# A planner that books VectorE's and GpSimd's shared memory ports, in a two-layer hybrid decoder step on one core

## The chip, the cores and the metric

The kernel runs on one core of one Trainium2 chip. The core has five engines, each with an instruction queue of its own that it works off in order: TensorE (PE in the profile; its weight loads are PEld), VectorE (DVE), ScalarE (ACT), GpSimd (POOL) and SyncE (SP), which here issues nearly all DMAs. Engines wait for each other through semaphores. SBUF is the memory that all of them read and write; PSUM holds TensorE's results. The metric is the device time of one execution in microseconds.

## The reference, cut to what matters

One inference step of two layers, for a prompt of 2048 rows (1024 wide, float32) and for 8 samples with a paged cache of 2048 earlier rows each. The weights are shared.

```python
# layer 0 (even): spatial gating || stick-breaking attention
h = x @ w_in_even;  u, v, gate_a, q, k, vb, gate_b = split(h)
out_a = gelu(u) * (tril(w_sp) @ standardize(gelu(v)) + b_sp) * silu(gate_a)       # chunks of 128 rows
z = q @ k.T / 8;  att = sigmoid(z) * exp(sum of log_sigmoid(-z) over later keys)  # keys < query
out_b = (att @ vb) * silu(gate_b)
# layer 1 (odd): indexer-selected attention || multi-scale pooling
h = x @ w_in_odd; q, kv, q_idx, k_idx, w_idx, gate_c, p, gate_d = split(h)
index = sum_h relu(q_idx[h] @ k_idx.T) * w_idx[h];  sel = top_k(index, 256)        # per query row
out_c = softmax(q @ k[sel].T / 8 + rel_bias) @ v[sel] * silu(gate_c)
out_d = ((mean of p over the last 2, 4, 8, 16 rows - p) @ w_grp) * scale * silu(gate_d)
# both layers
x = layer_norm(alpha * x + concat(out_1, out_2) @ w_out, g, b)
```

It returns both sets of rows and the new cache entries.

## The kernel before

**The work.** The prompt is cut into four blocks of 512 rows. Every projection is made in three matmuls of split operands (high x high, low x high, high x low: L671 to L673, and L1066 to L1068 for the output projection). The splits are made on the chip: ScalarE copies the high half (L597, L584) and a subtraction gives the low half. For the weights (`load_w`, L592) GpSimd subtracts the first half of the columns and VectorE the second, both after the same copy (L600). Stick-breaking attention (`b_logits`) runs its product along the keys as a scan on VectorE (L975); where the layers overlap, GpSimd turns a tanh into a sigmoid (L966) and masks the diagonal (L971). Sparse attention (`c_logits`) adds a mask to the logits and takes their maximum in one VectorE instruction that reads PSUM (L1705), and GpSimd prepares a piece of that mask (L1690). The selection (`topk`) is a search in six rounds for each 128 query rows: counts over the whole row on ScalarE and VectorE (L1449, L1451), and between them some dozen VectorE instructions of one to eight elements (L1482 to L1499), each of which needs the one before. Layer norm scales on ScalarE (L1148), multiplies on GpSimd (L1149) and adds on VectorE (L1150). The samples' work is spread among all of that.

**The order.** `Body.run` writes the instructions in an order woven by hand from these pieces. The class `Order` then throws this order away and plans its own for each of the five queues. `gather` (L154) collects what depends on what and which tiles share a buffer. `cost` (L243) gives each instruction the time that it keeps its engine and the time until its result is there: from the table `BUSY`, by engine, output tile, operation and size, or else from a formula. `plan` (L407) simulates the chip: whenever an engine is free it takes the ready instruction of the lowest rank, and a result is seen by others `SEM` ns later. `latest` (L499) walks the finished plan backwards and gives the latest time at which each could start, which is the rank for the next plan. `settle` (L316) repeats that for each of three guesses, plays each plan through under a few drawn sets of durations (`draw` L341, `replay` L356) and keeps the one with the least sum. `keep` (L554) fixes it:

```python
for o in self.order.values():
    for a, b in zip(o, o[1:]):
        self.tc.add_manual_dep(self.ins[b], self.ins[a].name, info, reason="planned order")
```

`o` is one engine's order and `info` a dependency without a semaphore, so the plan's times are not enforced: each engine starts its next instruction as soon as its own waits are over. The planner before knows nothing of the ports that VectorE and GpSimd share. Its table holds what instructions took in a profile, with whatever delayed them.

Of the kernel before, what the change touches and what calls it, by code (L numbers as in the profile page):

```python
# [12 lines left out]
F32R = mybir.dt.float32r  # L13
# [6 lines left out]
PSUM = bass.MemoryType.PSUM  # L20
DRAM = bass.MemoryType.DRAM

P = 128
# [35 lines left out]
    "ACT g_s Activation 512": 515, "ACT s16 TensorCopy 128": 150, "ACT s_sg Activation 8": 95,  # L59
    "ACT zt Activation 128": 390, "ACT zt Activation 256": 500, "ACT zt Activation 384": 605,  # L60
    "DVE P TensorScalarPtr 256": 655, "DVE P TensorScalarPtr 384": 900, "DVE bf TensorCopy 1": 50,
    "DVE bfst TensorCopy 4": 145, "DVE fq TensorReduce 4": 60, "DVE fq TensorScalarPtr 1": 65,
    "DVE hT TensorCopy 8": 80, "DVE halo TensorCopy 16": 400, "DVE ix TensorScalarPtr 128": 465,
    "DVE ix TensorScalarPtr 256": 540, "DVE ix TensorScalarPtr 512": 810, "DVE kid TensorCopy 512": 345,
    "DVE kid TensorTensor 512": 640, "DVE ln_nb TensorScalarPtr 4": 70, "DVE ln_rs TensorTensor 1": 405,
    "DVE mk TensorScalarPtr 640": 940, "DVE mv BNStatsAggregate 6": 80, "DVE mx TensorScalarPtr 512": 665,
    "DVE nmax TensorReduce 1": 65, "DVE nmax TensorReduce 2": 70, "DVE nmax TensorReduce 3": 70,
    "DVE nmax TensorReduce 4": 70, "DVE nmax TensorReduce 5": 70, "DVE os_ TensorTensor 2": 225,
    "DVE os_ TensorTensor 4": 70, "DVE pg TensorTensor 512": 680, "DVE pl TensorScalarPtr 512": 835,
    "DVE pl TensorTensor 16": 410, "DVE ri Reciprocal 4": 90, "DVE rs_a TensorScalarPtr 4": 275,  # L70
    "DVE rs_t TensorScalarPtr 1": 60, "DVE rs_t TensorScalarPtr 4": 285, "DVE rs_t TensorTensor 1": 385,
    "DVE rs_t TensorTensor 3": 65, "DVE rs_t TensorTensor 4": 100, "DVE s_acc TensorTensor 8": 75,
    "DVE s_cd TensorScalarPtr 8": 115, "DVE s_cd TensorTensor 24": 125, "DVE s_lg TensorTensor 128": 210,
    "DVE s_mxp TensorReduce 1024": 1995, "DVE s_pl TensorReduce 120": 1190, "DVE s_pl TensorTensor 8": 390,
    "DVE s_pr TensorScalarPtr 128": 730, "DVE s_qb TensorScalarPtr 8": 285, "DVE s_rq TensorScalarPtr 8": 110,
    "DVE s_sg TensorScalarPtr 8": 75, "DVE s_sgm TensorScalarPtr 128": 390, "DVE s_tmp TensorTensor 408": 560,
    "DVE s_tr Memset 8": 40, "DVE s_u TensorTensor 8": 125, "DVE s_xm TensorScalarPtr 8": 620,
    "DVE tk_M TensorTensor 8": 170, "DVE tk_W TensorTensor 3": 110, "DVE tk_a TensorScalarPtr 1": 245,
    "DVE tk_b TensorScalarPtr 1": 65, "DVE tk_b1 TensorScalarPtr 1": 95, "DVE tk_b2 TensorScalarPtr 1": 125,
    "DVE tk_f TensorScalarPtr 1": 120, "DVE tk_f TensorTensor 1": 190, "DVE tk_fl TensorCopy 1": 55,  # L80
    "DVE tk_mg TensorScalarPtr 1": 65, "DVE tk_mv TensorScalarPtr 2": 500, "DVE tk_nn TensorScalarPtr 2": 110,
    "DVE tk_oh TensorTensor 4": 160, "DVE tk_okn TensorScalarPtr 5": 210, "DVE tk_pen TensorScalarPtr 3": 315,
    "DVE tk_sd TensorScalarPtr 1": 65, "DVE tk_sd TensorTensor 1": 180, "DVE tk_th TensorScalarPtr 1": 235,
    "DVE tk_tn TensorCopy 2": 305, "DVE tk_tn TensorReduce 16": 85, "DVE tk_tn TensorScalarPtr 3": 400,
    "DVE tk_u TensorScalarPtr 1": 130, "DVE tk_u3 TensorScalarPtr 3": 265, "DVE tk_wd Reciprocal 1": 75,
    "DVE vT TensorCopy 1": 65, "DVE va TensorScalarPtr 512": 580, "DVE vea0 TensorCopy 4": 965,
    "DVE vea2 TensorCopy 4": 530, "DVE vlast TensorCopy 1": 65, "DVE xres TensorTensor 512": 1045,
    "DVE xs_ln TensorTensor 512": 600, "POOL P TensorScalarAffineSelect 128": 415,
    "POOL P TensorScalarPtr 256": 420, "POOL P TensorScalarPtr 384": 530, "POOL dT TensorTensor 512": 1240,
    "POOL ix TensorScalarAffineSelect 128": 405, "POOL nm TensorTensor 128": 600,  # L90
    "POOL ol TensorTensor 512": 1360, "POOL s_tr TensorTensor 8": 260, "POOL tk_W TensorScalarPtr 1": 485,
    "POOL tk_b2 TensorScalarPtr 1": 385, "POOL tk_f TensorScalarPtr 1": 190, "POOL tk_isl TensorTensor 1": 205,
    "POOL tk_u TensorScalarPtr 1": 260, "POOL ws TensorTensor 513": 1875, "POOL ws TensorTensor 521": 1190,
    "POOL ws TensorTensor 525": 1205, "POOL ws TensorTensor 527": 1050,
    "POOL wsp TensorScalarAffineSelect 128": 255, "POOL xres TensorTensor 512": 1520,
# [3 lines left out]
class Order:  # L99
# [5 lines left out]
    GUESSES = ((1.0, 150), (1.05, 150), (1.0, 0))  # L105
    ROUNDS, DRAWS, SPREAD = 5, 2, 0.12
    TAIL = {"ACT": 100, "POOL": 60, "DVE": 75}
# [135 lines left out]
    def cost(self, n):  # L243
# [38 lines left out]
        if e == "POOL":  # L282
            c = {"TensorTensor": 150 + (2.85 if i.outs[0].dtype == F32R else 2.4) * k, "Iota": 50 + 0.9 * k, "Memset": 40}.get(i.opcode, 330 + 0.9 * k)
            return c, c + 60
        if getattr(i, "is_tensor_tensor_scan", False):
            c = 130 + 2.3 * k
        elif k <= 16:
            c = 120 if len(full) < 2 and i.opcode != "TensorScalarPtr" else 190
        elif i.opcode == "TensorTensor" and not ps:
            c = 140 + 1.3 * k  # L290
        elif i.opcode == "TensorScalarPtr" and len(i.outs) > 1 and len(full) == 1:
            c = 150 + 1.05 * k
        elif i.opcode == "TensorScalarPtr" and not ps:
            c = 180 + 0.54 * k if len(full) == 1 else 160 + 1.1 * k
        else:
            c = 85 + 1.04 * k
# [18 lines left out]

    def settle(self):  # L316
# [7 lines left out]
        self.kinds = [self.kind(n) for n in range(N)]  # L324
        self.succ = [[] for _ in range(N)]
# [2092 lines left out]
```

## Time and profile before

| | |
|---|---|
| time, median of 3 runs | 2931.59 us (2930.24 to 2943.6) |
| the profiled execution | 2930.72 us, its span 2929.0 us |
| TensorE busy | 2726.8 us (93%) |
| VectorE busy | 2137.6 us (73%) |
| ScalarE busy | 1605.6 us (55%) |
| GpSimd busy | 1195.7 us (41%) |
| granted TensorE clock, mean | 0.970 |

The profile is of one execution. Busy time counts from an instruction's start to its end as the hardware recorded them. An instruction that has started and is then held up counts as busy, so VectorE's and GpSimd's busy time holds what they spend waiting for each other's ports. TensorE's matmuls overlap and their ends are modelled; its idle time is the time in which none runs. "PE z_c L1703 <- DVE mx L1705: 27.0, 15, 8.0" in the view of waits says that matmuls of line 1703, writing z_c, were held up 15 times by VectorE's instruction of line 1705, 27.0 us in all and 8.0 at most. The groups give busy us and mean ns of one, then the idle time of the engine before them and who ended it. The clock is the share of full speed that the chip granted TensorE; 0.5 is half speed.

### The profile page before, as it was taken

The numbers are of one execution on the slowest core, as the hardware profiler recorded it, in microseconds if no ns is written. First come the engines' busy times: TensorE is split into PE (matmuls) and PEld (weight loads), VectorE is DVE, ScalarE is ACT, GpSimd is POOL, SyncE is SP. The second block draws the span as 40 slices with busy tenths as digits, with TensorE's granted clock in tenths as the row PEclk, the third lists the DMA queues.
The fourth block names the chain that finished last, engine by engine and source line by source line (L and its number), as shares of the span: only waits on it lengthen the run. The fifth ranks groups of instructions, "written<-read, shape, count | busy, mean of one in ns | idle before, by whom it ended". The sixth has DMA issues, their size and how long they took to land. (4 is left out here: it accounts for less than half of the span.)

```text
span 2929.0 us, 52271 instructions
## 1 busy us (share of the span) xinstructions
PE 2726.8 (93%) x17490; PEld 2162.6 (74%) x17490; DVE 2137.6 (73%) x5297; ACT 1605.6 (55%) x3216; POOL 1195.7 (41%) x1300
## 2 busy tenths in 40 slices
PE   8999999989999999989799999998999999998986
PEld 6886777757767777668477667777767788887875
DVE  2376559756766977538887978887888877988865
ACT  2433334434444354435566677775776667776853
POOL 2223336422323543245453624446422555445342
PEclk9999999999999999989899999999989999998998
DMA  7556866775585668453475545435565655766452
GB/s 216 163 178 201 264 192 208 220 251 181 175 247 174 220 197 295 137 161 117 143 212 142 156 132 154 122 91 146 154 184 156 197 176 166 232 210 196 122 191 68
DMA packets 536591, 523.50 MB, mean 179 GB/s; under 512 B 43183, under 2 KB 408904, under 8 KB 536287
## 3 DMA queue, kind: packets, MB, share of 16 engines
q1 hardware_dynamic: 526439, 484.29, 55.2%
q0 software_dynamic: 9856, 35.66, 3.8%
q8 instruction: 138, 2.26, 0.3%
q14 instruction: 158, 1.29, 0.1%
HBM read 430.27 MB, written 89.73 MB: 178 GB/s over the span
## 5 line engine op out<-in xcount | busy, mean ns | idle before, releaser
L600 POOL TENSOR_TENSOR wl<-wr,wh 128x512 fp32r<-128x512 f32 x260 | 414.3, 1594 | 888.5 <-ACT wh L597 777.4
L671 PE MATMUL pp<-xh,wh 128*128 128x512 f32 (+1 forms) x1536 | 631.4, 414 | 23.0 <-DVE q_hl L590 9.1
L672 PE MATMUL pp<-xl,wh 128*128 128x512 f32 (+1 forms) x1536 | 617.7, 403 | 5.7 <-DVE xl L590 5.7
L673 PE MATMUL pp<-xh,wl 128*128 128x512 f32 (+1 forms) x1536 | 616.8, 402 | 0.7 <-POOL wl L600 0.7
L597 ACT CAST wh<-wr 128x1024 fp32r<-128x1024 f32 x260 | 269.9, 1038 | 383.4 <-PE pp L672 168.2
L600 DVE TENSOR_TENSOR wl<-wr,wh 128x512 fp32r<-128x512 f32 x260 | 222.3, 855 | 202.3 <-ACT wh L597 187.7
L671 PEld LDWEIGHTS pp<-xh,wh 128*128 128x128 f32 (+1 forms) x1536 | 288.7, 189 | 99.6 <-issue 19.8
L672 PEld LDWEIGHTS pp<-xl,wh 128*128 128x128 f32 (+1 forms) x1536 | 290.0, 189 | 68.6 <-issue 12.3
L673 PEld LDWEIGHTS pp<-xh,wl 128*128 128x128 f32 (+1 forms) x1536 | 289.5, 188 | 68.4 <-issue 10.1
L1066 PE MATMUL pp_o<-wh,oh 128*128 128x256 f32 x1008 | 295.9, 297 | 17.1 <-ACT oh L584 11.6
L975 DVE TENSOR_TENSOR_SCAN P<-P,bfst 128x512 f32<-128x512 f32 x192 | 275.0, 1441 | 28.3 <-ACT P L968 23.1
L1068 PE MATMUL pp_o<-wh,ol 128*128 128x256 f32 x1008 | 288.5, 291 | 4.0 <-POOL ol L590 4.0
L1067 PE MATMUL pp_o<-wl,oh 128*128 128x256 f32 x1008 | 290.9, 291 | 0.3 <-POOL wl L600 0.3
L1703 PE MATMUL z_c<-ksc,qc 128*128 128x512 f32 (+3 forms) x816 | 226.3, 358 | 37.9 <-DVE mx L1705 27.0
L999 ACT COPY P<-ps_p 128x512 f32<-128x512 f32 (+1 forms) x320 | 165.7, 522 | 156.3 <-PE ps_p L998 144.1
L1721 ACT ACTIVATE zt<-zt,nmax 128x512 f32<-128x512 f32 (+3 forms) x320 | 209.0, 655 | 57.3 <-DVE nmax L1709 56.4
L1066 PEld LDWEIGHTS pp_o<-wh,oh 128*128 128x128 f32 x1008 | 194.7, 194 | 27.7 <-ACT oh L584 12.6
L1736 ACT COPY zt<-ps_pc 128x512 f32<-128x512 f32 (+3 forms) x320 | 163.3, 519 | 88.4 <-PE ps_pc L1734 83.6
L961 PE MATMUL z<-ks,q 128*128 128x512 f32 (+3 forms) x640 | 196.2, 390 | 14.0 <-ACT r L1396 3.0
L1449 ACT ACTIVATE mk<-ix,tk_tn 128x512 int8<-128x512 f32 (+13 forms) x140 | 183.3, 1309 | 35.3 <-DVE tk_tn L1499 16.6
L1068 PEld LDWEIGHTS pp_o<-wh,ol 128*128 128x128 f32 x1008 | 193.3, 194 | 10.2 <-POOL ol L590 5.5
L1067 PEld LDWEIGHTS pp_o<-wl,oh 128*128 128x128 f32 x1008 | 195.6, 194 | 5.2 <-issue 1.8
(456 smaller groups left out, 5830.4 us busy)
## 6 DMA issues: line engine op xcount, KB each, us to landing
pg<-cache_b_kv SPq DMA_DIRECT2D x256, 256.0 KB
wr<-w_in_even SPq DMA_DIRECT2D x112, 512.0 KB
wr<-w_in_odd SPq DMA_DIRECT2D x76, 512.0 KB
wr<-w_out SPq DMA_DIRECT2D x68, 512.0 KB
ks<-ksc SPq DMA_DIRECT2D x80, 256.0 KB
ksc<-kcs SPq DMA_DIRECT2D x80, 256.0 KB
q<-qsc SPq DMA_DIRECT2D x64, 256.0 KB
qc<-qcs SPq DMA_DIRECT2D x128, 128.0 KB
```

Of the source, the lines that this page charges most:

```text
L597: nc.scalar.copy(hi, raw)
L600: e.tensor_tensor(lo[:, c], raw[:, c], hi[:, c].bitcast(F32), op=OP.subtract)
L671: nc.tensor.matmul(ps[:m], wh[:, kt, :m], xh[kt], start=a, stop=False)
L672: nc.tensor.matmul(ps[:m], wh[:, kt, :m], xl[kt], start=False, stop=False)
L673: nc.tensor.matmul(ps[:m], wl[:, kt, :m], xh[kt], start=False, stop=b)
L961: nc.tensor.matmul(z[:, :n], q2[:, c, t * P:(t + 1) * P].bitcast(F32R), ks[:, :n].bitcast(F32R), start=c == 0, stop=c == 1)
L975: nc.vector.tensor_tensor_scan(r, r, r, initial=ini, op0=OP.mult, op1=OP.bypass)
L1066: nc.tensor.matmul(ps[:, :256], oh[:, tt], wh[:, k], start=a, stop=False)
L1067: nc.tensor.matmul(ps[:, :256], oh[:, tt], wl[:, k], start=False, stop=False)
L1068: nc.tensor.matmul(ps[:, :256], ol[:, tt], wh[:, k], start=False, stop=b)
L1703: nc.tensor.matmul(z[:, :n], q2[:, c, jj % 2, :].bitcast(F32R), kk, start=c == 0, stop=c == 1)
L1721: nc.scalar.activation(zt, zt, AF.Exp, bias=nmx, accum_out=st["rs"][:, h, c:c + 1])
```

## The change

`port` is new. It says of each VectorE and GpSimd instruction whether it needs the shared ports: on GpSimd, whatever reads SBUF; on VectorE, what reads two tensors from SBUF (scans too), and copies and tensor-with-scalar operations from SBUF to SBUF with one output and more than one element. `plan` and `replay` keep a time `hold` for each of the two engines, up to which its running port instruction has the ports (its busy time less 60 ns). A port instruction of the other engine does not start before it. In `plan` the engine may take a ready instruction that needs no ports instead, if that ends at most 100 ns after the hold does.

The table and the formulas of `cost` are refitted to undisturbed durations; most small entries go away, since the formulas now cover them. `GUESSES` varies the hand-over time of the plan (200, 250 and 230 ns, the last with costs 4% up) where it varied costs and the price of a change between kinds of matmul. The replay, which still hands over in 200 ns, draws durations with a spread of 5% (12% before) and DMA times up to 1.15 (1.5 before). `settle` now keeps the `after` links (which tile follows which in a buffer) of the plan that it keeps.

No instruction is added or taken away, and the class `Body` is unchanged.

```diff
--- before.py
+++ after.py
@@ -56,43 +56,30 @@
 
 
 BUSY = {
...
-    "DVE mk TensorScalarPtr 640": 940, "DVE mv BNStatsAggregate 6": 80, "DVE mx TensorScalarPtr 512": 665,
...
-    "DVE tk_oh TensorTensor 4": 160, "DVE tk_okn TensorScalarPtr 5": 210, "DVE tk_pen TensorScalarPtr 3": 315,
...
-    "DVE vT TensorCopy 1": 65, "DVE va TensorScalarPtr 512": 580, "DVE vea0 TensorCopy 4": 965,
-    "DVE vea2 TensorCopy 4": 530, "DVE vlast TensorCopy 1": 65, "DVE xres TensorTensor 512": 1045,
...
-    "POOL P TensorScalarPtr 256": 420, "POOL P TensorScalarPtr 384": 530, "POOL dT TensorTensor 512": 1240,
-    "POOL ix TensorScalarAffineSelect 128": 405, "POOL nm TensorTensor 128": 600,
...
+    "ACT zt Activation 512": 710, "DVE P TensorScalarPtr 384": 840, "DVE bfst TensorCopy 4": 80,
...
+    "DVE tk_wd Reciprocal 1": 75, "DVE zt ISA 128": 210, "DVE zt ISA 256": 345,
+    "POOL P TensorScalarAffineSelect 128": 255, "POOL dT TensorTensor 512": 1000,
+    "POOL ix TensorScalarAffineSelect 128": 255, "POOL nm TensorTensor 128": 390,
+    "POOL s_tr TensorTensor 8": 155, "POOL tk_W Memset 1": 60, "POOL tk_W TensorScalarPtr 1": 250,
...
 }
 
 
@@ -102,9 +89,10 @@
     ENGINES = {"PE": "PE", "DVE": "DVE", "Activation": "ACT", "Pool": "POOL", "SP": "SP"}
     SEM, DMA_START, DMA_END, RATE = 200, 700, 1500, 280.0
     TILED = 150
-    GUESSES = ((1.0, 150), (1.05, 150), (1.0, 0))
-    ROUNDS, DRAWS, SPREAD = 5, 2, 0.12
-    TAIL = {"ACT": 100, "POOL": 60, "DVE": 75}
+    GUESSES = ((1.0, 200), (1.0, 250), (1.04, 230))
+    ROUNDS, DRAWS, SPREAD = 5, 2, 0.05
+    TAIL = {"ACT": 100, "POOL": 45, "DVE": 75}
+    OTHER, RELEASE, SLACK = {"DVE": "POOL", "POOL": "DVE"}, 60, 100
 
     def __init__(self, tc, lags):
         self.tc, self.lags = tc, lags
@@ -280,20 +268,17 @@
             c = 70 + (0.82 if ps else 0.87) * k if i.opcode == "TensorCopy" else 70 + 0.83 * k if ps else 200 + 0.93 * k
             return c, c + 100
         if e == "POOL":
-            c = {"TensorTensor": 150 + (2.85 if i.outs[0].dtype == F32R else 2.4) * k, "Iota": 50 + 0.9 * k, "Memset": 40}.get(i.opcode, 330 + 0.9 * k)
-            return c, c + 60
+            c = {"TensorTensor": 15 + 2.4 * k, "Iota": 50 + 0.9 * k, "Memset": 40}.get(i.opcode, 180 + 0.78 * k)
+            return c, c + 45
+        ptr = sum(getattr(x, "bass_ap", None) is not None and self.size(x) == 1 for x in i.ins) if k > 1 else 0
         if getattr(i, "is_tensor_tensor_scan", False):
-            c = 130 + 2.3 * k
-        elif k <= 16:
-            c = 120 if len(full) < 2 and i.opcode != "TensorScalarPtr" else 190
-        elif i.opcode == "TensorTensor" and not ps:
-            c = 140 + 1.3 * k
-        elif i.opcode == "TensorScalarPtr" and len(i.outs) > 1 and len(full) == 1:
+            c = 40 + 2.23 * k
+        elif i.opcode == "TensorScalarPtr" and not ps and len(full) == 1 and len(i.outs) == 1:
+            c = 65 + 0.54 * k + 60 * ptr
+        elif i.opcode == "TensorScalarPtr" and len(i.outs) > 1:
             c = 150 + 1.05 * k
-        elif i.opcode == "TensorScalarPtr" and not ps:
-            c = 180 + 0.54 * k if len(full) == 1 else 160 + 1.1 * k
         else:
-            c = 85 + 1.04 * k
+            c = 65 + 1.04 * k + 60 * ptr
         return c, c + 75
 
     def out(self, n):
@@ -312,6 +297,23 @@
             return None
         return "t" if i.is_transpose else "h" if self.halves(n) else "r" if i.ins[0].dtype == F32R else "f"
 
+
+    def port(self, n):
+
+        i, e = self.ins[n], self.eng[n]
+        if e not in self.OTHER or "DMA" in i.opcode or type(i).__name__ == "BassTileConditionalBlock":
+            return False
+        sb = lambda x: self.space(x) not in (None, DRAM, PSUM)
+        ins = [x for x in i.ins if getattr(x, "bass_ap", None) is not None]
+        full = [x for x in ins if self.size(x) > 1]
+        if e == "POOL":
+            return any(map(sb, ins))
+        if i.opcode == "TensorTensor" or getattr(i, "is_tensor_tensor_scan", False):
+            return sum(map(sb, ins)) > 1
+        if i.opcode == "TensorScalarPtr" and len(full) > 1:
+            return sum(map(sb, full)) > 1
+        return (i.opcode in ("TensorScalarPtr", "TensorCopy") and len(i.outs) == 1 and self.size(i.outs[0]) > 1
+                and all(map(sb, (*full, i.outs[0]))))
 
     def settle(self):
 
@@ -322,27 +324,32 @@
             self.costs[g] = busy, busy + 170
         self.dma = [e is not None and "DMA" in i.opcode for e, i in zip(eng, self.ins)]
         self.kinds = [self.kind(n) for n in range(N)]
+        self.ports = [self.port(n) for n in range(N)]
         self.succ = [[] for _ in range(N)]
         for n, d in enumerate(self.dep):
             for m in d:
                 self.succ[m].append(n)
         self.links()
         draws, mid, best = [self.draw(k) for k in range(self.DRAWS)], self.costs, None
-        for by, self.TILED in self.GUESSES:
+        sem = self.SEM
+        for by, near in self.GUESSES:
             self.costs = [(b * by, l * by) if e in self.TAIL else (b, l) for e, (b, l) in zip(eng, mid)]
+            self.SEM = near
             self.plan(list(range(N)))
             for _ in range(self.ROUNDS):
+                self.SEM = near
                 self.plan(self.latest())
+                self.SEM = sem
                 x = sum(self.replay(c) for c in draws)
                 if best is None or x < best[0]:
-                    best = x, self.order
-        self.costs, self.order = mid, best[1]
+                    best = x, self.order, self.after
+        self.costs, (_, self.order, self.after) = mid, best
 
     def draw(self, seed):
 
         rng, out = random.Random(seed), []
         for e, d, (b, l) in zip(self.eng, self.dma, self.costs):
-            f = rng.gauss(1.0, self.SPREAD) if e in self.TAIL and not d else rng.uniform(0.9, 1.5) if d else 1.0
+            f = rng.gauss(1.0, self.SPREAD) if e in self.TAIL and not d else rng.uniform(0.9, 1.15) if d else 1.0
             out.append((b if d else b * f, l * f))
         return out
 
@@ -383,12 +390,17 @@
                 s = max(s, x)
             return s
 
-        ready = [(0.0, n) for n in range(N) if not left[n]]
+        ready, hold = [(0.0, n) for n in range(N) if not left[n]], dict.fromkeys(self.OTHER, 0.0)
         while ready:
             s, n = pop(ready)
+            if self.ports[n] and hold[self.OTHER[eng[n]]] > s:
+                push(ready, (hold[self.OTHER[eng[n]]], n))
+                continue
             count += 1
             if eng[n] is not None:
                 busy, lat = cost[n]
+                if self.ports[n]:
+                    hold[eng[n]] = s + max(40, busy - self.RELEASE)
                 if eng[n] == "PE" and n in seq and self.kinds[n] != self.kinds[seq[n]]:
                     s += 150 if "h" in (self.kinds[n], self.kinds[seq[n]]) else 0
                 start[n], idle[n], done[n] = s, s + busy, s + lat
@@ -407,7 +419,7 @@
     def plan(self, rank):
 
         N, eng, push, pop = len(self.ins), self.eng, heapq.heappush, heapq.heappop
-        cost, kinds, succ = self.costs, self.kinds, self.succ
+        cost, kinds, succ, ports, hold = self.costs, self.kinds, self.succ, self.ports, dict.fromkeys(self.OTHER, 0.0)
         left, tiles, home = [len(d) for d in self.dep], [[] for _ in range(N)], {}
         for g, ts in self.tags.items():
             for t in ts:
@@ -460,11 +472,24 @@
                 count += 1
                 for m in succ[n]:
                     release(m, now)
-            moved = False
+            moved, late = False, []
             for e, q in ready.items():
                 while q and idle[e] <= now:
-                    n = pop(q)[1]
+                    n, until = q[0][1], hold.get(self.OTHER.get(e), 0.0)
+                    if ports[n] and until > now:
+                        free_ = [x for x in q if not ports[x[1]] and now + cost[x[1]][0] <= until + self.SLACK]
+                        if not free_:
+                            late.append(until)
+                            break
+                        n = min(free_)
+                        q.remove(n)
+                        heapq.heapify(q)
+                        n = n[1]
+                    else:
+                        pop(q)
                     s, (busy, lat) = now, cost[n]
+                    if ports[n]:
+                        hold[e] = s + max(40, busy - self.RELEASE)
                     if e == "PE" and kinds[n] != kind:
                         s += self.TILED if "h" in (kinds[n], kind) else 0
                         kind = kinds[n]
@@ -492,6 +517,7 @@
                             push(back, (max(done[m] for m in u) + self.SEM, g, t))
             if not moved:
                 then = [q[0][0] for q in (due, back) if q] + [idle[e] for e in ready if ready[e]]
+                then = [x for x in then if x > now] + late
                 assert then or count == N
                 now = max([now] + [min(then)] if then else [now])
         return max(done)
```

More of the change, by code (lines that the diff above doesn't have):

```diff
@@ L58 @@
 BUSY = {
-    "ACT g_s Activation 512": 515, "ACT s16 TensorCopy 128": 150, "ACT s_sg Activation 8": 95,
+    "ACT g_s Activation 512": 515, "ACT mk Activation 1664": 1675, "ACT mk Activation 1792": 1785,
+    "ACT mk Activation 1920": 1885, "ACT mk Activation 2048": 1995, "ACT mk Activation 384": 585,
+    "ACT s16 TensorCopy 128": 150, "ACT s_sg Activation 8": 95, "ACT xres Activation 512": 715,
     "ACT zt Activation 128": 390, "ACT zt Activation 256": 500, "ACT zt Activation 384": 605,
-    "DVE P TensorScalarPtr 256": 655, "DVE P TensorScalarPtr 384": 900, "DVE bf TensorCopy 1": 50,
@@ L62 @@
[L62 to L65, printed above, removed]
-    "DVE mk TensorScalarPtr 640": 940, "DVE mv BNStatsAggregate 6": 80, "DVE mx TensorScalarPtr 512": 665,
@@ L67 @@
[L67 to L81, printed above, removed]
@@ L82 @@
-    "DVE tk_oh TensorTensor 4": 160, "DVE tk_okn TensorScalarPtr 5": 210, "DVE tk_pen TensorScalarPtr 3": 315,
-    "DVE tk_sd TensorScalarPtr 1": 65, "DVE tk_sd TensorTensor 1": 180, "DVE tk_th TensorScalarPtr 1": 235,
-    "DVE tk_tn TensorCopy 2": 305, "DVE tk_tn TensorReduce 16": 85, "DVE tk_tn TensorScalarPtr 3": 400,
-    "DVE tk_u TensorScalarPtr 1": 130, "DVE tk_u3 TensorScalarPtr 3": 265, "DVE tk_wd Reciprocal 1": 75,
-    "DVE vT TensorCopy 1": 65, "DVE va TensorScalarPtr 512": 580, "DVE vea0 TensorCopy 4": 965,
@@ L87 @@
-    "DVE vea2 TensorCopy 4": 530, "DVE vlast TensorCopy 1": 65, "DVE xres TensorTensor 512": 1045,
-    "DVE xs_ln TensorTensor 512": 600, "POOL P TensorScalarAffineSelect 128": 415,
-    "POOL P TensorScalarPtr 256": 420, "POOL P TensorScalarPtr 384": 530, "POOL dT TensorTensor 512": 1240,
-    "POOL ix TensorScalarAffineSelect 128": 405, "POOL nm TensorTensor 128": 600,
-    "POOL ol TensorTensor 512": 1360, "POOL s_tr TensorTensor 8": 260, "POOL tk_W TensorScalarPtr 1": 485,
-    "POOL tk_b2 TensorScalarPtr 1": 385, "POOL tk_f TensorScalarPtr 1": 190, "POOL tk_isl TensorTensor 1": 205,
@@ L93 @@
-    "POOL tk_u TensorScalarPtr 1": 260, "POOL ws TensorTensor 513": 1875, "POOL ws TensorTensor 521": 1190,
-    "POOL ws TensorTensor 525": 1205, "POOL ws TensorTensor 527": 1050,
-    "POOL wsp TensorScalarAffineSelect 128": 255, "POOL xres TensorTensor 512": 1520,
+    "ACT zt Activation 512": 710, "DVE P TensorScalarPtr 384": 840, "DVE bfst TensorCopy 4": 80,
+    "DVE hT TensorCopy 8": 80, "DVE kid TensorCopy 512": 345, "DVE ln_mv BNStatsAggregate 12": 120,
+    "DVE mk TensorScalarPtr 1280": 1590, "DVE mk TensorScalarPtr 640": 880, "DVE os_ TensorTensor 2": 75,
@@ new lines @@
+    "DVE rcn Reciprocal 64": 475, "DVE ri Reciprocal 4": 90, "DVE rs_t TensorScalarPtr 4": 80,
+    "DVE rs_t TensorTensor 4": 80, "DVE s_X TensorTensor 136": 940, "DVE s_cd TensorScalarPtr 8": 85,
+    "DVE s_lg TensorTensor 1024": 2190, "DVE s_mxp TensorReduce 1024": 2030, "DVE s_own Memset 512": 405,
+    "DVE s_pr Memset 1": 135, "DVE s_qb TensorScalarPtr 8": 90, "DVE s_ri Reciprocal 64": 455,
+    "DVE s_rk TensorScalarPtr 8": 560, "DVE s_th TensorScalarPtr 64": 1105, "DVE s_tmp TensorTensor 136": 460,
@@ new lines @@
+    "DVE s_tr Memset 8": 165, "DVE tk_M TensorTensor 8": 80, "DVE tk_W TensorTensor 3": 75,
+    "DVE tk_a TensorScalarPtr 1": 100, "DVE tk_b1 TensorScalarPtr 1": 95, "DVE tk_b2 TensorScalarPtr 1": 125,
+    "DVE tk_f TensorScalarPtr 1": 120, "DVE tk_oh TensorTensor 4": 75, "DVE tk_okn TensorScalarPtr 5": 85,
+    "DVE tk_th TensorScalarPtr 1": 135, "DVE tk_tn TensorScalarPtr 2": 85, "DVE tk_tn TensorScalarPtr 3": 200,
+    "DVE tk_tt TensorScalarPtr 1": 185, "DVE tk_u TensorScalarPtr 1": 125, "DVE tk_u3 TensorScalarPtr 3": 150,
@@ new lines @@
+    "DVE tk_wd Reciprocal 1": 75, "DVE zt ISA 128": 210, "DVE zt ISA 256": 345,
+    "POOL P TensorScalarAffineSelect 128": 255, "POOL dT TensorTensor 512": 1000,
+    "POOL ix TensorScalarAffineSelect 128": 255, "POOL nm TensorTensor 128": 390,
+    "POOL s_tr TensorTensor 8": 155, "POOL tk_W Memset 1": 60, "POOL tk_W TensorScalarPtr 1": 250,
+    "POOL tk_b2 TensorScalarPtr 1": 265, "POOL tk_isl TensorTensor 1": 155, "POOL tk_tt Memset 1": 60,
+    "POOL wl TensorTensor 144": 460, "POOL ws TensorTensor 521": 1015, "POOL ws TensorTensor 525": 1020,
@@ L96 @@
+    "POOL ws TensorTensor 527": 1030,
 }
```

## The prediction

> **What bounds the kernel now.** I read the page first, then the stages, then TensorE's waits, then the two engines that the change speaks of.
>
> ```profile
> span 2929.0 us, 52271 instructions
> ...
> PE 2726.8 (93%) x17490; PEld 2162.6 (74%) x17490; DVE 2137.6 (73%) x5297; ACT 1605.6 (55%) x3216; POOL 1195.7 (41%) x1300
> ...
> PEclk9999999999999999989899999999989999998998
> ```
>
> TensorE is the bound: it is idle for 2929.0 - 2726.8 = 202.2 us. The change adds no work and takes none away, so all that it can win is a part of these 202.2 us and of what the lowered clock costs. The view of the cores gives the mean granted clock:
>
> ```profile
> core 0: 2929.0 us, clock 0.970
> ```
>
> At 0.970, 3% of 2929.0 = 88 us of full-speed time were not granted. The stages (columns: length, busy us of each engine, clock, DMA) show where both lie:
>
> ```profile
> 0.00:20.00 20.00, 11.66 (x42) 8.54 (x42) 6.60 (x34) 6.29 (x11) 6.74 (x20) 1.00 0.90 263
> 20.00:400.00 380.00, 362.56 (x2059) 286.49 (x2060) 195.39 (x392) 139.05 (x272) 114.93 (x119) 0.99 0.67 198
> 400.00:1400.00 1000.00, 956.73 (x5359) 734.36 (x5359) 687.70 (x1100) 428.87 (x803) 397.27 (x409) 0.98 0.65 199
> 1400.00:2700.00 1300.00, 1203.38 (x8328) 965.32 (x8325) 1098.38 (x3330) 895.06 (x1857) 598.44 (x689) 0.96 0.56 166
> 2700.00:2915.00 215.00, 192.51 (x1707) 167.91 (x1705) 147.35 (x439) 134.86 (x274) 74.28 (x62) 0.96 0.39 122
> 2915.00:2929.00 14.00, 0.00 (x0) 0.00 (x0) 2.13 (x4) 1.52 (x2) 4.06 (x3) 0.50 0.51 172
> ```
>
> Length less PE busy is TensorE's idle time: 8.3, 17.4, 43.3, **96.6**, 22.5 and 14.0 us. The fourth stage, 1400 to 2700 us, holds almost half of it. There VectorE is busy 1098 of 1300 us (84%), GpSimd 598 (46%), and the clock is 0.96. In the stage before, VectorE is at 69% and TensorE idles for 4%. The first and last stages are the start and the end of the program.
>
> TensorE's waits (us in total, times, longest us):
>
> ```profile
> PE z_c L1703 <- DVE mx L1705: 27.0, 15, 8.0
> PE pp_o L1066 <- ACT oh L584: 11.6, 4, 8.2
> PE ps_sk L2184 <- DVE s_lg L2191: 9.4, 5, 3.3
> PE pp L671 <- DVE q_hl L590: 9.1, 4, 6.3
> PE ps_x L647 <- DMA xc<-x: 8.8, 5, 3.0
> PE pp L671 <- ACT xh L584: 8.2, 6, 4.4
> PE ps_w L719 <- POOL wsp L716: 6.2, 3, 3.1
> PE pp L672 <- DVE xl L590: 5.7, 2, 4.8
> ```
>
> No wait is regular. The largest, attention logits waiting for a PSUM bank that VectorE's mask-and-max (L1705) must empty, is 15 waits of which one took 8.0 us: VectorE was late, now and then. These are the places where the order written by the planner and the chip ran apart. The DMA row and the wsp row (the start) have nothing to do with the ports: 15.0 us that I leave alone.
>
> **Is VectorE late because of GpSimd?** This is the chip at the longest of these waits, from the timelines of VectorE, GpSimd and TensorE (start, us, engine, line):
>
> ```profile
> 2650.24 9.18 DVE L1483 TENSOR_TENSOR tk_oh<-tk_okn 128x4 f32<-128x4 f32 x1
> ...
> 2660.00 0.15 DVE L1485 TENSOR_TENSOR tk_M<-tk_tn,tk_oh 128x8 f32<-128x8 f32 x1
> ...
> 2668.13 1.07 DVE L1150 TENSOR_TENSOR xres<-xres,lnb 128x512 f32<-128x512 f32 x1
> ...
> 2670.62 0.68 DVE L1150 TENSOR_TENSOR xres<-xres,lnb 128x512 f32<-128x512 f32 x1
> ```
>
> ```profile
> 2654.47 4.92 POOL L1149 TENSOR_TENSOR xres<-xres,lng 128x512 f32<-128x512 f32 x4
> ...
> 2666.94 1.72 POOL L1513 TENSOR_TENSOR r<-ix,r 128x512 f32<-128x512 f32 x1
> ```
>
> ```profile
> 2660.82 1.22 PE L1703 MATMUL z_c<-ksc,qc 128*128 128x512 f32 x2 [7.96 <-DVE mx L1705]
> ```
>
> A subtraction of four elements a row took 9.18 us; its neighbour of eight took 0.15. It ended when GpSimd's unbroken run of multiplies (four of 1.23 us shown) ended at 2659.4, and the bank that TensorE wanted was queued behind it on VectorE: 7.96 us idle. The layer norm's addition shows the usual size: 0.68 us by itself, 1.07 when it starts before GpSimd's subtraction ends (2666.94 + 1.72 = 2668.66).
>
> [...]
>
> **The change part by part.** It issues the same 52271 instructions: no DMA, wait or tile differs. What changes is the order on each of the five queues, through three things.
>
> (1) The cost table. Old costs are averages with the blocking in them; new ones are undisturbed. In groups by line and shape (busy us, mean ns):
>
> ```profile
> L600 POOL TENSOR_TENSOR wl<-wr,wh 128x512 fp32r<-128x512 f32 x256 | 411.8, 1609 | 876.7 <-ACT wh L597 765.6 <-DMA pg<-cache_b_kv 23.8 <-issue 22.8
> ```
>
> ```profile
> L600 DVE TENSOR_TENSOR wl<-wr,wh 128x512 fp32r<-128x512 f32 x256 | 220.8, 862 | 197.1 <-ACT wh L597 182.5 <-PE pp L673 8.3 <-DMA lnb<-ln_b 3.4
> L1150 DVE TENSOR_TENSOR xres<-xres,lnb 128x512 f32<-128x512 f32 x64 | 65.0, 1030 | 6.4 <-POOL xres L1149 4.8 <-DMA wr<-w_in_even 1.6
> L1485 DVE TENSOR_TENSOR tk_M<-tk_tn,tk_oh 128x8 f32<-128x8 f32 x140 | 42.8, 311 | 13.4 <-DVEq L1535 12.4 <-DVE tk_oh L1483 0.5
> L1483 DVE TENSOR_TENSOR tk_oh<-tk_okn 128x4 f32<-128x4 f32 x70 | 26.4, 378 | 0.5
> ```
>
> The weight's low half (L600) is split between both engines and both start on the same ScalarE copy. One stretch where they meet and one where most do not (min/median/max ns):
>
> ```profile
> L600 DVE TENSOR_TENSOR wl<-wr,wh x4: 691/692/693, 302.7 to 326.9; 128x512 fp32r<-128x512 f32 x4
> L600 POOL TENSOR_TENSOR wl<-wr,wh x4: 1773/1798/1802, 302.8 to 326.9; 128x512 fp32r<-128x512 f32 x4
> ```
>
> ```profile
> L600 POOL TENSOR_TENSOR wl<-wr,wh x4: 1293/1379/1729, 1603.7 to 1638.5; 128x512 fp32r<-128x512 f32 x4
> L600 DVE TENSOR_TENSOR wl<-wr,wh x3: 673/677/691, 1606.2 to 1635.0; 128x512 fp32r<-128x512 f32 x3
> ```
>
> So blocking costs GpSimd 256 x (1609 - 1293) = 81 us here, and VectorE 256 x (862 - 673) = 48 us here, 64 x (1030 - 680) = 22 us in L1150, 140 x (311 - 150) = 23 us in L1485 and, taking its neighbour's 0.15 us, 70 x (378 - 150) = 16 us in L1483. That is 109 us of VectorE from four groups; there are many smaller ones, so 109 us is a lower bound on its stretching. The new formula puts L600 on GpSimd at 15 + 2.4 x 512 = 1244 ns busy, 1289 with the tail of 45, against 1293 seen. The table is right for an undisturbed instruction.
>
> (2) The exclusion, in the plan, in its replay and nowhere else. A ready port instruction waits in the plan while the other engine holds the ports, and VectorE is handed an instruction that needs none (L1705's, which reads PSUM, is one) if that fits. On the chip it works only through the order: `keep` ties each instruction to the one before it on its own engine, and nothing ties VectorE to GpSimd. What is queued behind a moved instruction is the rest of its engine's queue; nobody waits longer by construction.
>
> (3) Margins: the plan is now drawn with 200 to 250 ns per hand-over and the best of the plans is chosen under a spread of 5% instead of 12%. Their price has no row. Below nothing, they could lose the tolerance that the wide spread gave; above, they could win by an order that fits better. I take 0, since the trace has no row that either end is near.
>
> **The sum.** What can be had is TensorE's idle time in the stage of 1400 to 2700 us, 96.6 us, between none of it and all of it. Of the eight rows of waits, those of L1703, L2184 and L672 (42.1 us) end on VectorE, and the one that I followed is the ports' doing. But VectorE stays at (1098 - 109) / 1300 = 76% or more even if all of the 109 us lay in this stage, and a queue that full goes on being late sometimes. I take half: **48 us**. In the three stages around it that are neither start nor end (17.4 + 43.3 + 22.5 = 83.2 us) VectorE has slack, and I take 0; the ends are 0 and a quarter, 21 us.
>
> The clock comes on top. Of 88 us not granted, 7 belong to the last 14 us at 0.50; the other 81 go with 188 us of idle time, 0.43 us for each. 48 x 0.43 = **21 us**. Sum: 48 + 21 = 69 us. The profiled execution took 2930.7 us (1.7 us outside its span), 0.9 us below the median 2931.6, so both serve as base: 2931 - 69 = **2862 us**, 2.4% faster.
>
> The ends: all of 96.6 gives 96.6 x 1.43 = 138 us, 2793; the quarter of the other stages would give 30 more, 2763. None of it gives 2931.
>
> **The rivals.**
>
> *The exclusion stays on paper.* With no wait between the two engines, whoever is ready starts, and L600 alone releases both from one copy 256 times. Then the two meet as often as now and the new order is as good as the old: 2917 to 2946, centre 2930. For it: the change adds no semaphore. Against it: GpSimd is idle 59% of the time, mostly for inputs that come at the same point of the order each time, so that order does set when it runs.
>
> [...] Nothing in the trace of before can tell how often a planned separation would survive.
>
> *VectorE runs late against a plan that is now too tight* (slower). If the stretching stays at 109 us or more while the plan books undisturbed times, VectorE falls behind in the stage where it is at 84%, and L1703 waits for its bank more often. The old averages had paid for that in advance. Price: half as much idle again in that stage, 48 x 1.43 = 69 us, 3000; none, 2931; I take two thirds, 46 us: 2977. It decides as soon as the means of L600 and L1150 on VectorE stay at 862 and 1030 ns.
>
> *Nearly everything goes.* Idle time may feed on itself, since a half-speed clock makes TensorE late for others; with all of the stage gone and up to the quarter of the rest, 2763 to 2820, centre 2793. Against it: ScalarE's rows (11.6, 8.2) and the DMA's 8.8 are no port's.
>
> **How the numbers follow.** The forecast, 2820 to 2915 with 2862 likeliest, gets 0.53. Nearly everything 0.14, on paper only 0.16, too tight 0.17. A measurement tells 0.5% (15 us) from no change: faster 0.53 + 0.14 = 0.67, same 0.16, slower 0.17. The range is 2785 to 2955: below it lies about a third of the 0.14, above it about two thirds of the 0.17, together 0.16. The forecast's own range is 2820 to 2915.
>
> **What would show it.** VectorE's busy time falls from 2137.6 to about 2000 us and GpSimd's from 1195.7 to about 1100. L600 falls to about 1450 ns on GpSimd and 750 on VectorE, L1150 to 800; no operation of a few elements takes 9 us. TensorE's idle time goes from 202 to about 150 us and its clock to about 0.977, with the gain between 1400 and 2700 us. I am wrong if those means fall and TensorE's idle time does not (the blocking was covered), or if they stay and the time falls (then the margins or the luck of another order did it).

## The result

The changed kernel takes 2887.45 us (median of 4 runs, 2884.95 to 2894.34) against 2935.50 us of the kernel before beside it. The ratio is 0.9838, 95% interval 0.9806 to 0.9869: 1.6% faster, where 2.4% was forecast, and inside the forecast's range of 2820 to 2915 us. The profiled execution took 2884.95 us, 45.8 us less than the one before. Its page, and its row in the view of the cores:

```profile
span 2883.2 us, 52225 instructions
...
PE 2720.8 (94%) x17490; PEld 2168.1 (75%) x17490; DVE 2033.2 (71%) x5297; ACT 1604.5 (56%) x3216; POOL 1168.3 (41%) x1300
```

```profile
core 0: 2883.2 us, clock 0.970
```

TensorE's busy time hardly moves (2726.8 to 2720.8). Its idle time falls from 202.2 to 162.4 us, by 39.8. The clock stays at 0.970. VectorE is busy 104 us less, GpSimd 27 us less. The prediction said that the same 52271 instructions are issued; the page counts 52225. The working instructions of the four engines are the same in number. The difference is semaphore and register instructions, which go with the order (VectorE has 666 semaphore instructions, 723 before).

Stages by the clock on the wall no longer hold the same work, so I cut both profiles at the first and the last indexer matmul (z_i, L1393 before, L1419 after). Columns as before (length, busy us of PE, PEld, DVE, ACT, POOL, clock, DMA share, GB/s); first the kernel before, then the changed one:

```profile
0.00:1295.80 1295.80, 1240.03 (x6807) 952.75 (x6807) 815.48 (x1334) 522.29 (x962) 468.86 (x480) 0.99 0.67 204
1295.80:2649.40 1353.60, 1255.70 (x8697) 1009.70 (x8697) 1127.96 (x3411) 912.04 (x1912) 618.90 (x727) 0.96 0.56 163
2649.40:2929.00 279.60, 231.11 (x1989) 200.16 (x1987) 194.12 (x553) 171.32 (x343) 107.96 (x94) 0.92 0.43 138
```

```profile
0.00:1283.70 1283.70, 1241.41 (x6801) 955.22 (x6802) 775.42 (x1334) 521.58 (x963) 443.46 (x483) 0.99 0.68 206
1283.70:2613.70 1330.00, 1246.93 (x8656) 1008.76 (x8656) 1075.76 (x3400) 910.88 (x1913) 618.28 (x722) 0.96 0.56 165
2613.70:2883.20 269.50, 232.46 (x2037) 204.12 (x2035) 182.00 (x563) 172.08 (x341) 106.56 (x97) 0.94 0.47 149
```

The stages are shorter by 12.1, 23.6 and 10.1 us, and TensorE's idle time in them falls by 13.5, 14.8 and 11.4 us (55.8 to 42.3, 97.9 to 83.1, 48.5 to 37.0). The gain is spread over the whole program. The last stage here starts at 2649.4 us, so 12.0 us of the 96.6 that the prediction had in its stage of 1400 to 2700 lie in it. Cut instead where as many matmuls have started as at the prediction's bounds, its stage falls from 96.6 to 79.3 us, by 17.3, and all the others together by 22.5: the picture is the same.

TensorE's waits in the changed kernel, and the groups that answer to those of the prediction (L626 is L600 of before, L1176 is L1150, L1511 is L1485, L1509 is L1483):

```profile
PE pp_o L1092 <- DVE xres L1097: 12.2, 10, 4.7
PE z_c L1729 <- DVE mx L1731: 12.0, 12, 3.2
PE ps_x L673 <- DMA xc<-x: 11.8, 6, 6.8
PE pp L697 <- DVE q_hl L616: 8.5, 3, 4.7
PE ps_sk L2210 <- DVE s_lg L2217: 7.2, 2, 4.4
PE z_i L1419 <- DMA qi<-qis: 7.0, 1, 7.0
...
PE z_i L1419 <- ACT r L1422: 4.0, 6, 1.2
...
PE pp L697 <- ACT xh L610: 3.5, 6, 0.7
```

```profile
L626 DVE TENSOR_TENSOR wl<-wr,wh 128x512 fp32r<-128x512 f32 x256 | 218.6, 854 | 58.7 <-ACT wh L623 53.0 <-DMA otd<-c_sum 4.4 <-PE pp L699 1.2
L1176 DVE TENSOR_TENSOR xres<-xres,lnb 128x512 f32<-128x512 f32 x64 | 60.4, 961 | 8.6 <-POOL xres L1175 8.6
L1511 DVE TENSOR_TENSOR tk_M<-tk_tn,tk_oh 128x8 f32<-128x8 f32 x140 | 33.3, 249 | 3.5 <-DVEq L1561 2.9
L1509 DVE TENSOR_TENSOR tk_oh<-tk_okn 128x4 f32<-128x4 f32 x70 | 16.5, 236 | 0.8
```

```profile
L626 POOL TENSOR_TENSOR wl<-wr,wh 128x512 fp32r<-128x512 f32 x256 | 366.7, 1433 | 877.7 <-ACT wh L623 740.9 <-DVE rs_t L637 24.3 <-PE ps_p L1024 17.4
```

The wait for a logits bank (z_c) fell from 27.0 to 12.0 us. (z_c is a PSUM tile: in these 12 waits, 3.2 us at the longest, its matmuls stood until VectorE's L1731, which reads it, was done.) By the engine that ended them, all waits of TensorE together went like this: VectorE 84.8 to 67.0 us, ScalarE 55.8 to 25.7, GpSimd 11.2 to 9.7, DMA 19.8 to 33.5. The largest part of the gain is in waits that ScalarE ends, and ScalarE is neither of the two engines that the exclusion keeps apart.

The weights' low half shows how the plan separates the engines: VectorE used to stand idle 182.5 us for ScalarE's copy and then start together with GpSimd; now it stands 53.0 us, since its half comes later in its order. Taken in order, 115 of the 260 pairs of halves started within 0.1 us of each other before, and 42 do now. GpSimd's half is blocked less (1609 to 1433 ns), VectorE's hardly (862 to 854); GpSimd's other instructions take some 17 us more. What VectorE gains lies in the small operations of the selection (311 to 249 and 378 to 236 ns) and many like them: instructions that write at most 16 elements a row make up 85 of the 117 us by which its durations fall.

### The profile page after: what moved, and what is told of

It reads as the page before. It is cut to its first block, busy times and chain, and to the rows that moved or that the text cites. A ratio compares the mean times of both kernels' runs of the same rounds, so it can differ in the third digit from the quotient of the medians.

```text
span 2883.2 us, 52225 instructions
## 1 busy us (share of the span) xinstructions
PE 2720.8 (94%) x17490; PEld 2168.1 (75%) x17490; DVE 2033.2 (71%) x5297; ACT 1604.5 (56%) x3216; POOL 1168.3 (41%) x1300
## 5 line engine op out<-in xcount | busy, mean ns | idle before, releaser
L626 POOL TENSOR_TENSOR wl<-wr,wh 128x512 fp32r<-128x512 f32 x260 | 369.0, 1419 | 893.9 <-ACT wh L623 757.2
L697 PE MATMUL pp<-xh,wh 128*128 128x512 f32 (+1 forms) x1536 | 637.8, 418 | 15.1 <-DVE q_hl L616 8.5
L1001 DVE TENSOR_TENSOR_SCAN P<-P,bfst 128x512 f32<-128x512 f32 x192 | 264.0, 1382 | 33.6 <-ACT P L994 25.5
L626 DVE TENSOR_TENSOR wl<-wr,wh 128x512 fp32r<-128x512 f32 x260 | 219.8, 846 | 63.7 <-ACT wh L623 58.0
```

What stands on the lines that cost most here:

```text
L626: e.tensor_tensor(lo[:, c], raw[:, c], hi[:, c].bitcast(F32), op=OP.subtract)
L697: nc.tensor.matmul(ps[:m], wh[:, kt, :m], xh[kt], start=a, stop=False)
L1001: nc.vector.tensor_tensor_scan(r, r, r, initial=ini, op0=OP.mult, op1=OP.bypass)
```

## The experiments

The change has three parts: the table and formulas of `cost` (T), the exclusion (X), and the margins, that is guesses, spread and draws (M). Each run was measured beside the kernel before, on three chips in all (2938 to 2942 us for before), so ratios are compared, not times. The kernels with one or two parts keep the `after` links as the changed one does. They amount to the changed one with what the other parts replaced put back:

```diff
 without X
-        self.ports = [self.port(n) for n in range(N)]
+        self.ports = [False] * N
 without M
-    GUESSES = ((1.0, 200), (1.0, 250), (1.04, 230))
-    ROUNDS, DRAWS, SPREAD = 5, 2, 0.05
+    GUESSES = ((1.0, 150), (1.05, 150), (1.0, 0))
+    ROUNDS, DRAWS, SPREAD = 5, 2, 0.12
...
 without T: BUSY, TAIL and the formulas for POOL and DVE as before
-            c = {"TensorTensor": 15 + 2.4 * k, "Iota": 50 + 0.9 * k, "Memset": 40}.get(i.opcode, 180 + 0.78 * k)
+            c = {"TensorTensor": 150 + (2.85 if i.outs[0].dtype == F32R else 2.4) * k, "Iota": 50 + 0.9 * k, "Memset": 40}.get(i.opcode, 330 + 0.9 * k)
...
```

**T alone.**

> The new cost table and formulas alone; no exclusion, old guesses and spreads. Three theories stand for all the runs of the parts. Ports: the gain of 1.6% comes from VectorE and GpSimd meeting less, which the plan can only bring about if it knows of the ports. Costs and margins: any plan made with truer costs, or other margins, is better, ports or not. Luck: any new order moves the time by up to 1% either way. Ports expects 2935 to 2980 us here, VectorE's L600 mean at or over 862 ns and its busy time at or over 2130 us, since nothing keeps the two apart. Costs expects 2885 to 2910 us. Luck expects 2905 to 2965 us, with nothing to tell beforehand.

Measured: 3005.07 us, ratio 1.0217 (1.0185 to 1.0249). Slower, as Ports expected, and by more than the 1% that Luck was given. Ports' figures did not hold, though: the time is 25 us above its range, and VectorE's mean of L600 (857 ns) and busy time (2120.9 us) lie a little under its bounds.

```profile
PE 2763.1 (92%) x17490; PEld 2197.2 (73%) x17490; DVE 2120.9 (71%) x5297; ACT 1609.3 (54%) x3216; POOL 1189.1 (40%) x1300
```

```profile
PE z_c L1726 <- DVE mx L1728: 19.6, 13, 4.6
PE pp L694 <- DVE q_hl L613: 18.5, 7, 5.0
PE ps_sk L2207 <- DVE s_lg L2214: 11.9, 5, 6.6
...
PE pp L695 <- DVE xl L613: 9.4, 5, 4.3
```

VectorE is blocked nearly as much as before (2120.9 us busy), but the plan books undisturbed times; all the waits of TensorE that VectorE ends add up to 129 us, 85 before. This is the slower rival of the prediction.

**X alone.**

> The exclusion alone, on the old table, in which the blocking is counted already, and with the old guesses and spreads. Ports expects part of the gain, 2900 to 2925 us, with VectorE's busy time down from 2137.6 us by 30 to 100 us. Costs and margins expects 2930 to 2950 us. Luck expects 2905 to 2965 us with no tie to VectorE's busy time.

Measured: 2989.72 us, ratio 1.0193 (1.0156 to 1.0230). All theories missed the time.

```profile
PE 2765.8 (93%) x17490; PEld 2193.7 (74%) x17490; DVE 2013.3 (67%) x5297; ACT 1607.3 (54%) x3216; POOL 1120.7 (38%) x1300
```

```profile
PE z_c L1742 <- DVE mx L1744: 24.3, 20, 3.6
PE pp_o L1105 <- DVE xres L1110: 20.6, 7, 7.9
PE pp_o L1105 <- ACT oh L623: 10.0, 4, 8.5
```

The exclusion works here better than in the changed kernel: VectorE and GpSimd are busy 20 and 48 us less than there, the least so far. And yet TensorE is idle for 217 us, 202 before, and the clock takes another 34 us (table below). The waits that VectorE ends are 85 us, as before. Less blocking alone does not make the kernel faster.

**T and X.**

> Table and exclusion together, with the old guesses and spreads: the whole change but its margins. Ports expects nearly the whole gain, 2880 to 2905 us, VectorE's busy time 2010 to 2060 us. Costs expects the time of the table alone within 15 us. If the margins carry the gain, 2915 us or more.

Measured: 2892.82 us, ratio 0.9839 (0.9819 to 0.9860), VectorE busy 2037.8 us: the whole gain.

**M alone.**

> The new guesses of the hand-over time and the narrower draws alone, on the old table and without the exclusion. Ports expects no gain, 2925 to 2950 us, VectorE's busy time 2110 to 2150 us. Margins expects 2890 to 2910 us. Luck expects 2905 to 2965 us.

Measured: 2947.28 us, ratio 1.0028 (1.0016 to 1.0039), VectorE busy 2141.4 us. No gain from the margins, nor from the kept links.

**How far the plan may be off.** Since X alone had lowered the blocking and lost, the next run kept all of the change but booked the port instructions 15% too long.

```diff
+        self.costs = [(b * 1.15, l * 1.15) if p else (b, l) for p, (b, l) in zip(self.ports, self.costs)]
```

> The changed kernel with the planned cost of each instruction that needs the ports 15% up; exclusion, margins and all else as changed. The exclusion alone on the old table left the least blocking of all runs so far (VectorE busy 2013 us, its half of L600 794 ns) and yet took 1.9% longer than before. So two theories now: Truth, the time follows how well the plan's times for VectorE and GpSimd match the chip, and the blocking that is left matters less; Blocking, it follows the blocking that is left. Truth expects 2915 to 2960 us, on the way to the 2990 of the exclusion on inflated costs. Blocking expects 2870 to 2895 us, with VectorE's busy time at 2000 to 2030 us, since the plan keeps the two further apart.

Measured: 2921.14 us, ratio 0.9933 (0.9913 to 0.9953), VectorE busy 2025.4 us. Blocking is down as Blocking said, the time is where Truth said, by 6 us. Beside the next runs this alone would prove little.

**Luck.** The same planners with their guesses moved by an amount that means nothing:

```diff
 nudge_after, nudge_after_2
-    GUESSES = ((1.0, 200), (1.0, 250), (1.04, 230))
+    GUESSES = ((1.0, 206), (1.0, 256), (1.04, 236))
+    GUESSES = ((1.0, 194), (1.0, 244), (1.04, 224))
 nudge_before, nudge_before_2
-    GUESSES = ((1.0, 150), (1.05, 150), (1.0, 0))
+    GUESSES = ((1.006, 150), (1.056, 150), (1.006, 0))
+    GUESSES = ((0.994, 150), (1.044, 150), (0.994, 0))
```

> The changed kernel with its three guessed hand-over times 6 ns longer (206, 256, 236), which no theory says should matter but which gives other orders. It measures luck. If the gain belongs to the change, 2870 to 2905 us. If it is a lucky order, anywhere from 2890 to 2945 us.

Measured: 2915.58 us, ratio 0.9909 (0.9875 to 0.9943): 24 us more than the changed kernel's order measured beside it (2891.71 us, below), for 6 ns of hand-over. This lies in the range of a lucky order and outside that of the change: the luck of an order is worth some 0.8% here.

> The kernel before with the cost factors of its three guesses 0.006 up (1.006, 1.056, 1.006): again other orders and nothing else. If before is a fair draw of its planner, 2920 to 2955 us. If it was a lucky one, 2950 to 3000 us, and part of the harm of the single parts is only the loss of that luck.

Measured: 2910.84 us, ratio 0.9904 (0.9874 to 0.9934): faster than either case, by 1% for no reason that the planner knows of. One lucky order of the old planner equals one unlucky order of the new.

> The changed kernel with its three guessed hand-over times 6 ns shorter (194, 244, 224): a third draw of the same planner. So far its draws took 0.984 (as changed), 0.984 (without the new margins) and 0.991 (6 ns longer) of before. If the change as a whole is worth something beyond the luck of an order, 0.980 to 0.993 of before, VectorE busy at 2020 to 2075 us. If it is luck, 0.993 to 1.01.

Measured: 2903.32 us, ratio 0.9862 (0.9841 to 0.9884), VectorE busy 2042.9 us, both as expected if the change is worth something.

> The kernel before with the cost factors of its guesses 0.006 down (0.994, 1.044, 0.994): a third draw of the old planner, whose draws took 1, 1.003 (with the new margins) and 0.990. If the change is worth something, 0.993 to 1.01, VectorE busy at 2100 to 2150 us; at 0.985 or below, the gain of the change is within the old planner's luck.

Measured: 2941.72 us, ratio 0.9995 (0.9979 to 1.0012), VectorE busy 2122.0 us, again as expected in that case.

**Where the plans are chosen.**

```diff
 in replay
-            if self.ports[n] and hold[self.OTHER[eng[n]]] > s:
-                push(ready, (hold[self.OTHER[eng[n]]], n))
-                continue
...
```

> The changed kernel with the exclusion taken out of the replay that chooses among the 18 plans, and left in the plan that makes them. If the gain is in making orders that keep the two engines apart, 2880 to 2905 us. If it is in choosing the right one, 2905 to 2950 us.

Measured: 2891.71 us, ratio 0.9829 (0.9796 to 0.9862). The replay without the ports picked the same plan: the profiles show the same order on all five queues, but for one neighbouring pair on VectorE (a memset and an addition). So the gain does not need the ports in the choice, and this is a second measurement of all but the same program (0.9838 and 0.9829). Of the 18 plans that are made, `settle` replays 15; the first of each guess is not judged.

**The two halves once more**, with the new margins as a second draw:

> The new table and the new margins without the exclusion: a second draw of undisturbed costs in a plan that does not know of the ports. Truth expects 1.010 to 1.03 of before (1.022 with the old margins). If that first one was bad luck, 0.985 to 1.005.

Measured: 3006.45 us, ratio 1.0244 (1.0204 to 1.0285).

> The exclusion and the new margins on the old table, in which the blocking is counted already: a second draw of that. Truth expects 1.008 to 1.03 of before (1.019 with the old margins), with VectorE's busy time again near 2010 us. If the first one was bad luck, 0.985 to 1.005.

Measured: 2999.96 us, ratio 1.0201 (1.0179 to 1.0222), VectorE busy 2003.4 us, the least of all runs.

Together, each with the idle time of TensorE (span less busy) and the time that the clock did not grant (span times 1 less the mean clock), in us, and the sums of TensorE's waits that VectorE and ScalarE ended:

| parts | ratio to before | VectorE busy | TensorE idle | clock lost | waits ended by VectorE | by ScalarE |
|---|---|---|---|---|---|---|
| none (before) | 1 | 2137.6 | 202 | 88 | 85 | 56 |
| none, nudged | 0.990, 1.000 | 2105.9, 2122.0 | 179, 208 | 99, 106 | 78, 82 | 39, 41 |
| M | 1.003 | 2141.4 | 217 | 100 | 108 | 47 |
| T | 1.022 | 2120.9 | 241 | 126 | 129 | 43 |
| T, M | 1.024 | 2136.3 | 242 | 123 | 136 | 28 |
| X | 1.019 | 2013.3 | 217 | 122 | 85 | 61 |
| X, M | 1.020 | 2003.4 | 221 | 135 | 90 | 60 |
| T, X | 0.984 | 2037.8 | 170 | 90 | 64 | 30 |
| T, X, M (the change) | 0.984 | 2033.2 | 162 | 86 | 67 | 26 |
| T, X, M, nudged | 0.991, 0.986 | 2068.3, 2042.9 | 180, 169 | 99, 102 | 74, 67 | 32, 27 |
| T, X, M, port costs 15% up | 0.993 | 2025.4 | 178 | 120 | 74 | 37 |

Three things follow. First, span less idle less lost clock is 2625 to 2644 us in all fourteen profiles. It stays within 19 us: the work of TensorE hardly changes, and idle time and clock carry nearly all of the difference. (The 18 to 37 us of lost clock that fall into idle time count in both.) Second, T costs 2.2 to 2.4% without X and gains about 3.4% with it; X costs 2% without T and gains 3.7 to 4.0% with it. The parts are worth something only together. They fail in different ways: T alone in waits that VectorE ends, X alone mostly in clock. Third, the four draws with T and X average 0.986, the four with neither 0.998. So about 1.2% belongs to the change, by the scatter of the draws give or take 0.8%, and 0.4% of the measured 1.6% to the order that was drawn; the best draw of the old planner (0.9904) and the worst of the new (0.9909) touch. Between these two groups of four, the waits that VectorE ends fall by 20 us on average and those that ScalarE ends by 17, and those that a DMA ends rise by 10.

## Why the prediction was right, and where it was not

**The direction held, its cause in part.** VectorE and GpSimd block each other: VectorE's L1176, 668 ns at the shortest in the changed kernel, took 5.08 us once beside GpSimd (last section), and GpSimd's L600, 1293 ns at the shortest in the prediction's second stretch, took 1798 ns in the middle of its first, where both halves ran at once. "Ports" is the change's name for what they block each other over; the profiles show who was held up and for how long, not by what, and no run tried `port`'s list of who needs them. An order without any wait between them does keep them further apart: the rival "stays on paper" is out, since in all eight profiles with X VectorE is busy 2003 to 2068 us, in all six without it 2106 to 2141. TensorE's idle time falls by 39.8 us, where the sum had 48. But only 17.8 us of that are waits that VectorE ended, and 30.1 are waits that ScalarE ended, which the prediction called "no port's"; waits for DMAs rose by 13.7. Whether ScalarE is in time because VectorE is, or because the whole order fits better, no run tells apart.

**The clock's term, 21 us, was worth 2.** Its step was "0.43 us for each" us of idle time. Lost clock went from 88 to 86 us while idle time fell by 40; with X alone it rose by 34 while idle time rose by 15. In these runs it did not go with the sum of idle time (M and X alone both have 217 us of it, and lose 100 and 122), but with how it is bunched (last section): the changed kernel falls to half speed 27 times, before 23, and spends 50 of the clock's steps there, before 52. The step also counted twice: of the lost clock before, 34 us fell into TensorE's idle time itself, which the first term had already. The 6.0 us of the gain that are not idle time are TensorE's busy time, and the clock's 2 are part of them.

**The place was wrong.** The step "VectorE has slack, and I take 0" gave nothing outside the middle, where 25 of the 39.8 us came from; and half of the middle's idle time was 48 where 14.8 came. The two errors nearly cancel, so that 40 is near 48 is luck. VectorE busy 69% of a stage was not slack enough: my guess, which no run isolates, is that one blocked instruction delays what stands behind it there too, as the 9.18 us delayed L1705 in the stage at 84%. Of the eight rows of waits the prediction counted three that end on VectorE, 42.1 us; the row of q_hl (9.1 us) is a fourth, 51.2 us in all. The 48 do not rest on it.

**Which instructions get relief was half right.** L600 on GpSimd was forecast at 1450 ns and has 1433. VectorE's L600 (750 forecast, 854) and L1150 (800 forecast, 961) stay blocked, GpSimd's busy time falls to 1168 and not 1100, VectorE's to 2033 and not 2000. So "It decides as soon as the means of L600 and L1150 on VectorE stay at 862 and 1030 ns" was a poor sign: they nearly stayed, and the kernel is faster.

**The slower rival is real.** Stretched work against a plan with undisturbed costs is what T without X does, 2.2 and 2.4%, where the rival's price was 46 us (1.6%). The margins at 0 were right (0.9839 without them, 0.9838 with).

**What the prediction did not see.** It treated blocking as the cause of idle time, so that less of it must be faster. X on the old table has the least blocking of all and is 2% slower: that plan counts the blocking twice, in costs that hold it already and in the exclusion. The four combinations of T and X fit one reading: TensorE waits where the plan's times for the other engines are wrong, in either direction. The distance between planned and real starts was not measured, so this reading is argued from the combinations, and not shown by itself. The run with port costs 15% up does not decide it, since 0.993 is within the luck of an order of 0.991. X alone falls to half speed 35 times and spends 72 steps there (23 and 52 before); why its idle time is spread so is not settled either.

## What to carry to other kernels

Where a planner fixes the order, its costs and its rules must describe the same machine: undisturbed durations belong with a rule for what disturbs them, averages under load with none, and here mixing the two cost more (about 2%) than the right pair saved (about 1.2%). Before a new plan is credited with a per cent, draw a few neighbours of the old and the new one by nudging a setting that means nothing. For TensorE, count the long gaps, since in this kernel those cost clock as well: after a step of 3.41 us that was busy less than 30%, the next ran at half speed in 313 of 313 cases (next section).

## What the runs showed of the hardware

**A VectorE instruction can be held up through several GpSimd instructions in a row.** The 9.18 us of the prediction were no accident of the kernel before. In the changed one, the timeline of VectorE, then GpSimd, then TensorE:

```profile
2088.57 5.08 DVE L1176 TENSOR_TENSOR xres<-xres,lnb 128x512 f32<-128x512 f32 x1
2093.58 0.21 DVE L2109 SCALAR_TENSOR_TENSOR s_s<-ps_sl,s_wq 128x64 f32<-128x64 f32 x1
```

```profile
2087.49 1.25 POOL L2200 DMA_INDIRECT s_pg<-cache_c_kv,s_rq  x1 [0.16 <-issue]
2088.76 1.28 POOL L1175 TENSOR_TENSOR xres<-xres,lng 128x512 f32<-128x512 f32 x1
2090.00 0.66 POOL L1716 TENSOR_TENSOR nm<-nm,mk 128x256 f32<-128x256 f32 x1
2090.63 2.48 POOL L1175 TENSOR_TENSOR xres<-xres,lng 128x512 f32<-128x512 f32 x2
```

```profile
2093.85 1.11 PE L2100 MATMUL ps_sk<-idf,s_kp 128*128 128x128 f32 x4 [3.59 <-DVE s_s L2109]
```

The addition starts at 2088.57, while GpSimd issues an indirect DMA (until 2088.74), and then waits through four more GpSimd instructions, until 2093.11. TensorE is idle for 3.59 us behind it. The 9.18 us look the same: an indirect DMA, then seven instructions without a break from 2650.75 on, two subtractions (L590) and five multiplies. In the fourteen profiles 84 VectorE instructions, 2 to 9 a run, took over 2 us longer than the shortest of their kind, all beside such a run of GpSimd; 51 of them began during an indirect DMA. X alone has them too: an addition of 9.09 us, with TensorE idle for 3.63 us behind it. By its code the plan lets the engines alternate in such a place; the chip here let GpSimd go on, through four instructions and through seven. This is what the exclusion does not describe. Why these 84 were held up for so long, and the others not, stays open.

**The clock changes in steps of 3.41 us, and the step after a mostly idle one nearly always runs at half speed.** In the kernel before and the changed one, all records of the clock but the last of each (98 of 100) last a whole number of 3.413 us. The kernel before, around its longest wait, cut at the clock's own steps (length, PE busy, clock, DMA):

```profile
2648.38:2651.79 3.41, 3.41 (x28) 1.00 0.51 144
2651.79:2655.21 3.42, 0.90 (x5) 1.00 0.50 176
2655.21:2658.62 3.41, 0.00 (x0) 0.50 0.00 0
2658.62:2662.04 3.42, 1.23 (x3) 0.50 0.00 0
2662.04:2665.45 3.41, 3.41 (x17) 0.50 0.27 79
2665.45:2668.86 3.41, 3.17 (x27) 1.00 0.20 56
```

A step in which TensorE was busy for 0.90 of 3.42 us is followed by one at half speed; the first full step (3.41) still runs at half speed, the next at full. Over all fourteen profiles, from the first record of the clock on, the step after one busy less than 30% ran at half speed in 313 of 313 cases, after 30 to 50% in 205 of 226, after 50 to 60% in 81 of 189, after 60 to 90% in 184 of 973, and after over 90% in 76 of 10265 (in 75 of these 76 the step of over 90% was itself at half speed). So in these profiles idle time that gathered to over half of one step was followed by half speed in 518 of 539 cases, and 10 to 40% of a step in 184 of 973.
